# Rotating queries and keys straight out of PSUM and normalising them afterwards, with a shorter lag behind the products

## The chip, the cores and the metric

The kernel runs on one core of a Trainium2 chip, as one launch. The metric is the device time of the launch in microseconds (us). TensorE (PE in the profile) multiplies matrices out of SBUF into PSUM, which has eight banks of 512 f32 columns by 128 partitions; VectorE (DVE) and ScalarE (ACT) read PSUM and SBUF; GpSimd (POOL) works in SBUF; SyncE (SP) issues the DMAs.

## The reference

A two-layer encoder on 1024 tokens of width 1024, f32 throughout. Layer 0 mixes tokens by grouped-query attention (16 query heads, 4 key/value heads, 64 wide), layer 1 by a pooling mixer; each layer then has cross-attention to 256 memory tokens and a gated MLP. The change lies in the start of layer 0's attention alone:

```python
qkv = h @ w_qkv
q = rmsnorm(q, q_gain)            # per token and head: q * rsqrt(mean(q*q) + eps) * gain
k = rmsnorm(k, k_gain)
q = apply_axial_rope(q, cos, sin) * (HEAD_DIM ** -0.5)
k = apply_axial_rope(k, cos, sin) # out = stack([x1*c - x2*s, x2*c + x1*s])
scores = einsum(q, k); p = softmax(scores); o = einsum(p, v)
```

The norm of a token and head is one number per 64 values, so that it commutes with the rotation: rotating first and scaling afterwards gives the same up to rounding. The gains are folded into the cos and sin tables.

## The kernel before, in words

Every f32 product is made as three products of halves (a high part and a low part of each operand, `mm3`, lines 755 to 757), so each operand that goes into TensorE has to be split: ACT writes the high part (`high`, L668), DVE subtracts it from the source and writes the low part (`low`, L671).

The attention of layer 0 has two stages, each planned by its own `Plan`. A `Plan` is a list scheduler: each operation is added with an engine, a cost, what it reads, what buffers it takes from which pool, and a due time. The due time of a TensorE operation is the sum of the TensorE costs ahead of it; the operations before it are due by that much earlier than their own lag; `late` sets a due time by hand. The plan then simulates the engines and writes the instructions in the order in which they would start. TensorE's order is the one in which its operations were added. On the chip every engine runs its own queue in that order and waits by semaphores, so a wrong guess of the plan shows as a wait, never as another order.

The first stage (QKV) makes eight key/value tiles, K0 to K7 (128 tokens each; 24 products of 512 columns), then 32 query tiles (128 tokens by 256 columns, four heads; 24 products of 256 columns, `plan_gemm`). Its PSUM is a pool "B" of six banks for products and turns, and two banks "A". Eight "peaks" (`plan_peaks`: two score products into pA, and DVE's maximum over them, `nm`, L802) for the first group of the loop stand between the query tiles. The weights of the next four heads come as four pieces in two halves by DMA and are split by ACT and DVE (`plan_weights`).

What follows a key or query product is `plan_head` (L1010 to L1056) and a turn. In the kernel before:
- `square` on ACT (L1016): squares of the bank, scaled by `first`, the token's own norm, into `sq`;
- `reduce` on DVE (L1020): sums of 64 into `ss`;
- `rstd` on POOL: mean and eps (L728, `ms`) and the power -1/2 (L730, `rs`);
- `scaled` on DVE (L1033): bank times `first` times `rs`, into an SBUF buffer `qn` (a `kr` for keys). This is the last read of the bank;
- `crossed` on DVE (L1040, two instructions): the buffer with its pairs swapped, times the sin table, into `rb`;
- `straight` on DVE (L1044): the buffer times the cos table, in place;
- `both` on POOL (L1048): the sum of the two, in place;
- the `turn` on PE (L1105 for queries, L1072 for keys): two transposes (four for keys K2 and up, which also turn the difference `dk` of two key tiles, made on POOL, L1066) into another bank, then the split by ACT and DVE (`put`).

A turn stands `LAG` products behind its own product in TensorE's order. The last `LATE` query tiles are not turned in this stage: their rotated queries stay in an SBUF buffer `scr`, and the loop turns them (`plan_late`, L1213).

The second stage (the loop) has 16 groups of scores (PE L796 into pS and DVE's maximum L802 for the next group's softmax shift; L1239 into pT), exponentials on ACT (L1246) and products with the values (L1281), with sums on DVE (L1290) and POOL (L1293). It uses all eight banks again: pS is banks 0 to 2, pT 3 to 6, pO 7, so that its first products wait until the first stage has read those banks for the last time. After it come the output product, the cross-attentions, the pooling mixer and the MLPs, which the change does not touch; most of the time lies there.

## Time and profile before

| what | before |
|---|---|
| time, median of 3 runs | 2417.65 us (2416.79 to 2420.77) |
| the profiled execution: its time | 2417.89 us |
| the profiled execution: its span | 2416.1 us, granted TensorE clock 0.997 |
| TensorE busy | 2388.5 us, 99% |
| DVE, ACT, POOL busy | 1885.5, 1180.3, 415.3 us |
| key products and their turns | to about 60 us from the span's start |
| query products and their turns | about 60 to 163 us |
| the loop begins | 172.1 us |

All times of the profile count from the span's start. In a timeline a row is one instruction, or several like ones in a run (`x6`): its start, its length, the engine, the line, what it writes and reads, the sizes, and in brackets how long the engine sat idle before it and who released it. Two neighbouring rows of an engine may overlap a little, since the next instruction starts while the last one drains. In a table of groups a row gives busy time and the mean length of one, then idle time in front of them. In a table of windows each engine has its busy time and instruction count per stretch; PEclk is the granted clock of TensorE, 1.00 at full speed.

### The profile page before, as it was taken

To read this page: it belongs to the slowest core of one execution; us is meant where nothing else is said; L and a number is where in the kernel's file an instruction comes from. 1 tells how busy PE (TensorE), PEld (TensorE's weight loads), DVE (VectorE), ACT (ScalarE), POOL (GpSimd) and SP (SyncE) were. 2 spreads that over 40 slices of the span, in tenths; PEclk is the share of its full clock that TensorE was granted. 3 is DMA by queue.
4 is the path that set the end of the run, shared out by engine and by line. 5 is a ranking of instruction groups with operands and counts; after the bars stand their busy time and mean duration, and the time that the engine had idled before them with its cause. 6 is when DMAs were issued, how large, how long until landed. Compare 5 with 4: busy or idle time off the path is not lost.

```text
span 2416.1 us, 33574 instructions
## 1 busy us (share of the span) xinstructions
PE 2388.5 (99%) x12281; PEld 1925.2 (80%) x12281; DVE 1885.5 (78%) x2691; ACT 1180.3 (49%) x1900; POOL 415.3 (17%) x458
## 2 busy tenths in 40 slices
PE   9989999999999999999999999999999999999998
PEld 7974445688998888888888888798888888888887
DVE  6779999549873798888888767987389888888875
ACT  7225555425552465555554427555255554555542
POOL 5746777500020000000000003011000000000001
PEclk9999999999999999999999999999999999999999
DMA  6000001335961233333387533695123332338752
GB/s 247 8 1 10 19 15 44 120 105 175 319 223 40 72 116 114 105 109 109 96 271 260 178 108 129 207 323 217 49 87 111 108 109 87 112 121 273 261 187 101
DMA packets 323297, 323.00 MB, mean 134 GB/s; under 512 B 32596, under 2 KB 253628, under 8 KB 323132
## 3 DMA queue, kind: packets, MB, share of 16 engines
q1 hardware_dynamic: 323132, 320.85, 41.1%
q8 instruction: 97, 1.59, 0.3%
q14 instruction: 68, 0.56, 0.1%
HBM read 233.30 MB, written 82.64 MB: 131 GB/s over the span
## 4 chain that ended last, share of the span: by engine, by line
PE 91%; issue 3%; DVE 3%; POOL 2%; DMA 1%; ACT 1%; SPq 0%; POOLq 0%; DVEq 0%; ACTq 0%
PE pB L755 23%; PE pB L756 23%; PE pB L757 23%; PE pO L1281 4%; PE pT L1239 3%; PE pA L757 3%; PE pA L755 3%; PE pA L756 3%; PE pS L796 2%; PE pB L324 1%; DVE R L671 1%; PE pS L1317 1%; PE pA L2293 0%; POOL rs L730 0%; POOL scr L1293 0%
## 5 line engine op out<-in xcount | busy, mean ns | idle before, releaser
L756 PE MATMUL pB<-R,R 128*128 128x512 f32 (+1 forms) x2860 | 1051.8, 368 | 0.2 <-DVE R L671 0.2
L755 PE MATMUL pB<-R,R 128*128 128x512 f32 (+1 forms) x2732 | 1022.6, 374 | 2.2 <-ACT R L668 0.8
L757 PE MATMUL pB<-R,R 128*128 128x512 f32 (+1 forms) x2728 | 1014.8, 372 | 1.3 <-DVE R L671 1.2
L756 PEld LDWEIGHTS pB<-R,R 128*128 128x128 f32 x2860 | 538.9, 188 | 88.5 <-DVE R L671 1.2
L755 PEld LDWEIGHTS pB<-R,R 128*128 128x128 f32 x2732 | 514.6, 188 | 96.3 <-ACT R L668 2.0
L757 PEld LDWEIGHTS pB<-R,R 128*128 128x128 f32 x2728 | 513.8, 188 | 91.8 <-DVE R L671 3.0
L668 ACT ACTIVATE R<-scr 128x512 fp32r<-128x512 f32 (+3 forms) x376 | 269.5, 744 | 235.2 <-DMA scr<-Gs 62.1
L671 DVE TENSOR_TENSOR R<-scr,R 128x512 fp32r<-128x512 f32 (+2 forms) x336 | 289.5, 889 | 25.1 <-ACT R L668 24.3
L728 POOL TENSOR_SCALAR ms<-ss 128x1 f32<-128x1 f32 (+1 forms) x92 | 25.7, 279 | 1645.1 <-ACT R L736 1279.5
L671 DVE TENSOR_TENSOR R<-X,R 128x512 fp32r<-128x512 f32 x258 | 175.5, 688 | 48.3 <-ACT R L668 47.9
L668 ACT ACTIVATE R<-X 128x512 fp32r<-128x512 f32 x258 | 160.9, 630 | 97.8 <-PE pB L756 48.3
L438 ACT COPY scr<-pB 128x512 f32<-128x512 f32 x156 | 91.1, 584 | 181.8 <-PE pB L757 174.6
L802 DVE TENSOR_REDUCE nm<-pS 128x1 f32<-128x512 f32 x240 | 153.2, 683 | 19.8 <-PE pS L796 18.3
L1246 ACT ACTIVATE X<-pT 128x1024 f32<-128x1024 f32 x128 | 125.3, 1023 | 79.7 <-PE pT L1239 74.4
L755 PE MATMUL pA<-R,R 128*128 128x512 f32 (+1 forms) x420 | 150.6, 359 | 0.0
L757 PE MATMUL pA<-R,R 128*128 128x512 f32 (+1 forms) x420 | 150.3, 358 | 0.0
L756 PE MATMUL pA<-R,R 128*128 128x512 f32 (+1 forms) x420 | 150.0, 357 | 0.0
L1281 PE MATMUL pO<-X,XV 128*64 128x512 f32 x512 | 123.8, 605 | 0.0
L1984 DVE TENSOR_TENSOR X<-pB,X 128x512 f32<-128x512 f32 (+1 forms) x109 | 74.7, 686 | 62.1 <-PE pB L757 61.3
L440 DVE TENSOR_TENSOR scr<-pB,scr 128x512 f32<-128x512 f32 x156 | 107.1, 687 | 11.8 <-PE pB L757 11.5
L1239 PE MATMUL pT<-R,R 64*128 64x512 f32 x768 | 105.5, 395 | 1.6 <-ACT X L1246 1.6
L1829 DVE SCALAR_TENSOR_TENSOR scr<-scr,conv 128x1023 f32<-128x1023 f32 x66 | 84.7, 1284 | 20.5 <-ACT scr L1824 18.6
(222 smaller groups left out, 2936.0 us busy)
## 6 DMA issues: line engine op xcount, KB each, us to landing
Gs<-X SPq DMA_DIRECT2D x105, 256.0 KB
X<-in_ffn_w_up SPq DMA_DIRECT2D x51, 512.0 KB
scr<-in_ffn_w_down SPq DMA_DIRECT2D x45, 512.0 KB
scr<-Gs SPq DMA_DIRECT2D x35, 512.0 KB
scr<-in_xattn_w_kv SPq DMA_DIRECT2D x32, 512.0 KB
scr<-Gs SPq DMA_DIRECT2D x42, 384.0 KB
XV<-in_ffn_w_up SPq DMA_DIRECT2D x31, 512.0 KB
Wt<-scr SPq DMA_DIRECT2D x44, 256.0 KB
```

Source lines behind the costliest of these rows:

```text
L438: self.nc.scalar.copy(out, p)
L440: self.nc.vector.tensor_tensor(out=out, in0=p, in1=out, op=OP.add)
L668: self.nc.scalar.activation(hi, src, AF.Copy)
L671: self.nc.vector.tensor_tensor(out=lo, in0=src, in1=hi.bitcast(F32), op=OP.subtract)
L755: mm(out, ah, bh, start=start, stop=False)
L756: mm(out, ah, bl, start=False, stop=False)
L757: mm(out, al, bh, start=False, stop=stop)
L802: nc.vector.tensor_reduce(NM[G][:, 2 * n + x.start:2 * n + x.stop], S, axis=AX.X, op=OP.max, negate=True)
L1239: nc.tensor.matmul(T[G, kt % 2][:, x * 512:(x + 1) * 512], left, right, start=first and (i, j) == (0, 0), stop=shifted or (not first and i ...
L1246: nc.scalar.activation(E[G, kt], T[G, kt % 2], AF.Exp)
L1281: nc.tensor.matmul(O[G][x * HD:(x + 1) * HD], V32[kt // 4][:, kt % 4, m // 4 * 2 + x], E[G, kt][:, x * 512:(x + 1) * 512], start=kt == 0, ...
L1829: nc.vector.scalar_tensor_tensor(c[:, 1:], u[:, :S - 1], self.cv[:, 0, j + f:j + f + 1], c[:, 1:], op0=OP.mult, op1=OP.add)
```

## The change

1. The head of a tile is put in another order. `crossed` and `straight` now read the product's bank (two sin products into `rb`, one cos product into `qn`), `both` adds them on POOL, and `scaled` comes last, in SBUF and in place, with `first` and `rs`. The bank is now read for the last time by `straight`, which does not wait for the norm. The mean and eps are made on DVE (`mean`, L727) instead of POOL; POOL keeps the power (L735) and the addition (L1052).
2. A turn stands three products behind its product (`LAG` 3).
3. Two query tiles instead of four are left to the loop (`LATE` 2): the first stage has 30 turns of queries instead of 28. For the two that are left, `scaled` too is done by the loop.
4. The peaks stand behind query tiles 5, 7, 9, 11, 13, 16, 22 and 25, counted from 0 (before: 10, 12, ... 24).
5. The low parts of the second halves of weight pieces 2 and 3 go from DVE to POOL (L974, 128x1024).
6. Due times and costs: the splits behind a query's turn get `late`, the loop's plan starts with the engines as busy as the first plan left them, the late tiles get other known times.

```diff
-QKV = (... QS[:9], *(it for n, q in enumerate(QS[9:]) for it in ([q, ("S", n // 2)] if n % 2 == 1 and n < 16 else [q])))
-LAG, LATE = 4, 4
+PEAKS = (5, 7, 9, 11, 13, 16, 22, 25)
+QKV = (... *(it for n, q in enumerate(QS) for it in ([q, ("S", PEAKS.index(n))] if n in PEAKS else [q])))
+LAG, LATE = 3, 2
...
+    def mean(self, on, ss, n, width):
+        ms = self.stat(n, "ms")[:ss.shape[0]]
+        on.tensor_scalar(ms, ss, 1.0 / width, EPS, op0=OP.mult, op1=OP.add)
+        return ms
...
-                    def low(raw=raw, g=g):
-                        self.low(h[:, 4 * g:4 * g + 4], l[:, 4 * g:4 * g + 4], at[raw])
+                    kind, engine = ("pool", nc.gpsimd) if g and piece > 1 else ("add", nc.vector)
+                    def low(raw=raw, g=g, engine=engine):
+                        engine.tensor_tensor(out=l[...], in0=at[raw], in1=h[...].bitcast(F32), op=OP.subtract)
...
                 def reduce():
                     nc.vector.tensor_reduce(at[ss], ...)
+                    at[ss] = self.mean(nc.vector, at[ss], 4, HD)
...
-                def scaled():
-                    nc.vector.scalar_tensor_tensor(q3(), x, first[:, t:t + 1], r, op0=OP.mult, op1=OP.mult)
                 def crossed():
-                    q5, b5 = (... for z in (at[qn], at[rb]))
+                    q5, b5 = (... for z in (at[b], at[rb]))
                 def straight():
-                    nc.vector.tensor_tensor(out=q3(), in0=q3(), in1=tabs[kind][:, t, 0]..., op=OP.mult)
+                    nc.vector.tensor_tensor(out=q3(), in0=at[b]..., in1=tabs[kind][:, t, 0]..., op=OP.mult)
+                def scaled(at=at):
+                    z = at[qn].rearrange("p (h c) -> p h c", h=4)
+                    nc.vector.scalar_tensor_tensor(z, z, first[:, t:t + 1], at[ss]..., op0=OP.mult, op1=OP.mult)
-                plan.add("add", 340, reduce, [sq], [ss], uses=[sq])
-                plan.add("scale", 2.9, rstd, [ss], [ss])
-                plan.add("add", 340, scaled, [b, ss], [qn], ..., [b])
-                plan.add("add", 490, crossed, [qn, tabkey], [rb], [("rb", rb)], [qn, *used])
-                plan.add("add", 360, straight, [qn, tabkey], [qn], uses=[qn, *used])
-                plan.add("scale", 2.4, both, [qn, rb], [qn] + ..., uses=[qn, rb])
+                plan.add("add", 490, crossed, [b, tabkey], [rb], [("rb", rb)], [b, *used])
+                plan.add("add", 400, straight, [b, tabkey, rb], [qn], ..., [b, *used])
+                plan.add("add", 440, reduce, [sq], [ss], uses=[sq])
+                plan.add("scale", 2.3, rstd, [ss], [ss], late=3.0 if deferred else None)
+                plan.add("scale", 1.7, both, [qn, rb], [qn], uses=[qn, rb], late=4.0 if deferred else None)
+                if deferred:
+                    finish[late.index(it)] = scaled
+                else:
+                    plan.add("add", 340, scaled, [qn, ss, ("first", t)], [qn] + ..., uses=[qn])
...
-            plan = Plan(R, {}, {"A": 3, "B": 2, "O": 1, ...})
+            plan = Plan(R, plan.over, {"A": 3, "B": 2, "O": 1, ...})
-            plan.known.update({("late", i): 3.0 + 2.5 * i for i in range(LATE)})
+            plan.known.update({("late", i): (0.5, 3.0)[max(i - LATE + 2, 0)] for i in range(LATE)})
+                plan.add("add", 340, lambda: at_late.update({i: finish[i]()}), [b], [b], uses=["late"], late=1.0)
                 plan.add("turn", 2, turn, [b], [(b, 0)], [("A", b)], ["late"])
```

Three places show what the order of instructions becomes. In the rows a number behind a name tells one buffer from another; pB, pS and pT are PSUM banks, sq, ms, rs, qn, kr, rb and scr are SBUF buffers.

The first is TensorE at the end of the first stage. Before, the last product goes to pB_2200, one turn follows, and the loop begins with pS_2303:

```order
L756 MATMUL pB_2200<-R5_72,R16_83 128x256
L757 MATMUL pB_2200<-R4_71,R17_84 128x256
L1105 MATMUL pB_2225<-ident_87,qn_2119 128x128 x2
L796 MATMUL pS_2303<-R0_67,R18_85 128x512
L796 MATMUL pS_2304<-R0_67,R18_85 128x512
L1239 MATMUL pT_2307<-R18_85,R0_67 128x512 x4
```

In the changed kernel the last product goes to pB_2224, two turns follow, and the loop begins with pS_2313:

```order
L761 MATMUL pB_2224<-R5_72,R16_83 128x256
L762 MATMUL pB_2224<-R4_71,R17_84 128x256
L1117 MATMUL pB_2265<-ident_87,qn_2168 128x128 x2
L1117 MATMUL pB_2270<-ident_87,qn_2217 128x128 x2
L801 MATMUL pS_2313<-R0_67,R18_85 128x512
L801 MATMUL pS_2314<-R0_67,R18_85 128x512
```

Two turns in place of one stand between the last product and the loop. By the placement of the banks pS_2303 lies in that of pB_2200, and waits for its `scaled`; pS_2313 lies in that of the last turn, pB_2270, and waits for its `low`, and pS_2314 in that of the last product, pB_2224.

The second is VectorE at the same place. Before, from the last tile's `reduce` (sq_2244) to the first maximum of the loop:

```order
L1020 TENSOR_REDUCE ss4_2246<-sq_2244 128x4
L671 TENSOR_TENSOR R11_78<-pB_2225,R11_78 128x2x128
L1033 SCALAR_TENSOR_TENSOR scr_2170<-pB_2127,first_113,rs_2253 128x256
L1040 TENSOR_TENSOR rb_2256<-scr_2170,tab_111 128x8x16 x2
L1044 TENSOR_TENSOR scr_2170<-scr_2170,tab_111 128x256
L1033 SCALAR_TENSOR_TENSOR scr_2170<-pB_2172,first_113,rs_2263 128x256
L1040 TENSOR_TENSOR rb_2266<-scr_2170,tab_111 128x8x16 x2
L1044 TENSOR_TENSOR scr_2170<-scr_2170,tab_111 128x256
L1033 SCALAR_TENSOR_TENSOR scr_2170<-pB_2200,first_113,rs_2273 128x256
L1040 TENSOR_TENSOR rb_2276<-scr_2170,tab_111 128x8x16 x2
L1044 TENSOR_TENSOR scr_2170<-scr_2170,tab_111 128x256
L802 TENSOR_REDUCE nm_2314<-pS_2303 128x1
```

In the changed kernel, the same stretch, from the last tile's `reduce` (sq_2268):

```order
L1027 TENSOR_REDUCE ss4_2276<-sq_2268 128x4
L727 TENSOR_SCALAR ms_2278<-ss4_2276 128x4
L1038 TENSOR_TENSOR rb_2282<-pB_2224,tab_111 128x8x16 x2
L672 TENSOR_TENSOR R12_79<-pB_2265,R12_79 128x2x128
L1048 TENSOR_TENSOR scr_2273<-pB_2224,tab_111 128x256
L672 TENSOR_TENSOR R12_79<-pB_2270,R12_79 128x2x128
L1211 MEMSET ones_2309 128x64
L807 TENSOR_REDUCE nm_2327<-pS_2313 128x1
```

The three `scaled` that stood behind the last `reduce`, each on an `rs` of its own from POOL, are gone from this place; two of them (of pB_2173 and pB_2224) stand twelve maxima later, in the loop. Two `low` of turns have come in.

The third is POOL in the key tiles: the tables for the keys (scr, from tab and gk), the powers rs of the first tiles, the first tokens' norms (first), and the first sums kr. Before:

```order
L899 TENSOR_TENSOR scr_370<-tab_111,gk_115 128x8x64
L906 TENSOR_TENSOR scr_370<-tab_111,gk_115 128x8x16 x2
L728 TENSOR_SCALAR ms_381<-ss4_368 128x4
L730 TENSOR_TENSOR rs_383<-ms_381,mh_92 128x4
L931 TENSOR_SCALAR ms_390<-ss_387 128x1
L932 TENSOR_TENSOR first_113<-ms_390,mh_92 128x1
L728 TENSOR_SCALAR ms_393<-ss4_377 128x4
L730 TENSOR_TENSOR rs_395<-ms_393,mh_92 128x4
L906 TENSOR_TENSOR scr_370<-tab_111,gk_115 128x8x16 x2
L1048 TENSOR_TENSOR kr_397<-kr_397,rb_438 128x256
```

In the changed kernel:

```order
L904 TENSOR_TENSOR scr_333<-tab_111,gk_115 128x8x64
L911 TENSOR_TENSOR scr_333<-tab_111,gk_115 128x8x16 x2
L936 TENSOR_SCALAR ms_373<-ss_370 128x1
L937 TENSOR_TENSOR first_113<-ms_373,mh_92 128x1
L911 TENSOR_TENSOR scr_333<-tab_111,gk_115 128x8x16 x2
L735 TENSOR_TENSOR rs_380<-ms_339,mh_92 128x4
L936 TENSOR_SCALAR ms_398<-ss_395 128x1
L937 TENSOR_TENSOR first_113<-ms_398,mh_92 128x1
L1052 TENSOR_TENSOR kr_389<-kr_389,rb_382 128x256
```

The tables now stand ahead of the first power, since `crossed` and `straight` need them before `scaled` needs the norm. On TensorE the first key tile's turn stands behind product K2 (before: behind K3, together with K1's).

More of the change, by code (lines that the diff above doesn't have):

```diff
@@ L40 @@
 QS = [(g, t) for g in range(2) for t in range(NT)] + [(2 + n // 4 % 2, n % 4 + n // 8 * 4) for n in range(2 * NT)]
[L41 to L42 removed]
+PEAKS = (5, 7, 9, 11, 13, 16, 22, 25)
+QKV = (*(("K", t) for t in range(NT)), *(it for n, q in enumerate(QS) for it in ([q, ("S", PEAKS.index(n))] if n in PEAKS else [q])))
+LAG, LATE = 3, 2
 QN = 4
@@ L779, in attention @@
         Q, OT, NM, ring = {}, [], {}, []
-        late = [(1, NKV - 1, t) for t in range(NT - LATE, NT)]
+        late, finish = [(1, NKV - 1, t) for t in range(NT - LATE, NT)], {}
         def rows(x):
@@ L1200, in attention @@
             T, E, O, acc, ON, RS = {}, {}, {}, {}, {}, {}
-            plan = Plan(R, {}, {"A": 3, "B": 2, "O": 1, "pt": 6, "scr": 6, "qm": 3, "half": len(R.freed)})
+            plan = Plan(R, plan.over, {"A": 3, "B": 2, "O": 1, "pt": 6, "scr": 6, "qm": 3, "half": len(R.freed)})
             plan.hold("qm", ("qm", 0))
```

43 lines of the change are left out of this document (22 added, 21 removed).

## The prediction

> **What bounds the kernel now.** I read the page first, then what TensorE waits for, then the stretch around the longest wait.
>
> ```profile
> PE 2388.5 (99%) x12281; PEld 1925.2 (80%) x12281; DVE 1885.5 (78%) x2691; ACT 1180.3 (49%) x1900; POOL 415.3 (17%) x458
> core 0: 2416.1 us, clock 0.997
> PE pS L796 <- DVE scr L1033: 9.0, 1, 9.0
> PE pB L1072 <- POOL dk L1066: 1.6, 2, 1.1
> PE pB L1190 <- POOL ident masks.py:199: 1.3, 1, 1.3
> PE pB L1072 <- POOL kr L1048: 0.6, 1, 0.6
> PE pS L796 <- DVE nm L802: 0.6, 2, 0.3
> ```
>
> TensorE is busy for all but 27.6 us of the span (2416.1 - 2388.5). The change leaves nearly all its matmuls in place, so it can win or lose only through TensorE's idle time, its granted clock, and a few turns. The last five rows are TensorE's waits (total, times, longest), four up to the start of the loop and one in its first 68 us: one of 9.0 us between the two stages, and 2.2 us on the keys (1.6 + 0.6). The wait for ident stands ahead of the first product and is not touched. The wait of 9.0 us in order of time, on TensorE, POOL and DVE:
>
> ```profile
> 162.73 0.38 PE L1105 MATMUL pB<-ident,qn 128*128 128x128 f32 x2
> 172.09 0.80 PE L796 MATMUL pS<-R,R 64*128 64x512 f32 x2 [8.97 <-DVE scr L1033]
> 166.73 1.01 POOL L730 TENSOR_TENSOR rs<-ms,mh 128x4 f32<-128x4 f32 x1
> 167.78 0.48 DVE L1033 SCALAR_TENSOR_TENSOR scr<-pB,first,rs 128x256 f32<-128x256 f32 x1 [2.21 <-POOL rs L730]
> 170.41 1.01 POOL L730 TENSOR_TENSOR rs<-ms,mh 128x4 f32<-128x4 f32 x1
> 171.46 0.48 DVE L1033 SCALAR_TENSOR_TENSOR scr<-pB,first,rs 128x256 f32<-128x256 f32 x1 [2.21 <-POOL rs L730]
> ```
>
> POOL and DVE hand the left-over tiles to each other, one per 3.68 us (171.46 - 167.78), and the loop's first bank is free only when the last `scaled` has read it. What the idle time does to the clock:
>
> ```profile
> 164.50:165.00 0.50, 0.00 (x0) 0.00 (x0) 0.47 (x3) 0.00 (x0) 0.00 (x0) 1.00 0.00 0
> 165.00:165.50 0.50, 0.00 (x0) 0.00 (x0) 0.47 (x2) 0.00 (x0) 0.00 (x0) 0.53 0.00 0
> 175.00:175.25 0.25, 0.25 (x5) 0.18 (x4) 0.23 (x1) 0.25 (x1) 0.00 (x0) 0.50 0.00 0
> 175.50:176.00 0.50, 0.50 (x8) 0.42 (x4) 0.50 (x2) 0.15 (x1) 0.00 (x0) 1.00 0.00 0
> 180.00:200.00 20.00, 19.57 (x111) 9.32 (x110) 18.75 (x29) 9.55 (x13) 8.76 (x4) 1.00 0.04 1
> ```
>
> The columns are length, busy PE, PEld, DVE, ACT, POOL, then the clock. It falls to 0.50 at about 165.0, 1.9 us after the last turn's end (162.73 + 0.38), and is full again at about 175.3, 3.2 us into the loop.
>
> **The change, part by part. The gap between the stages.** The durations of the new chain come from these rows (the first three from the old tail, the fourth a turn from the chain of waits, the others means over 62 to 160 us; L808 is the nearest row to the new `mean`, a DVE instruction on 8 columns):
>
> ```profile
> 162.61 0.29 PE L757 MATMUL pB<-R,R 128*128 128x256 f32 x1
> 162.94 0.47 ACT L1016 ACTIVATE sq<-pB,first 128x256 f32<-128x256 f32 x1 [2.34 <-PE pB L757]
> 163.44 0.42 DVE L1020 TENSOR_REDUCE ss<-sq 128x4 f32<-128x256 f32 x1 [2.33 <-ACT sq L1016]
> 159.81 0.22 PE pB L1105 x2
> L1040 DVE TENSOR_TENSOR rb<-qn,tab 128x128 f32<-128x128 f32 x56 | 15.1, 312 | 0.0
> L1044 DVE TENSOR_TENSOR qn<-qn,tab 128x256 f32<-128x256 f32 x28 | 12.4, 444 | 0.3
> L671 DVE TENSOR_TENSOR R<-pB,R 128x256 fp32r<-128x256 f32 x29 | 12.1, 416 | 0.0
> L808 DVE TENSOR_TENSOR nmr<-nm 128x8 fp32r<-128x8 f32 x1 | 0.2, 172 | 0.0
> L802 DVE TENSOR_REDUCE nm<-pA 128x2 f32<-128x1024 f32 x8 | 9.7, 1217 | 2.1 <-PE pA L796 2.1
> ```
>
> The last product ends at 162.90 (162.61 + 0.29); the loop begins 9.19 us later (172.09). In the new order, counted from the end of the last product: `square` and the start of `reduce` at 0.54 (163.44 - 162.90), `reduce` to 0.96, `mean` 0.17 to 1.15, `crossed` about 0.55 (two of 0.31 that overlap) to 1.7, a `low` 0.37, `straight` 0.42, the last `low` 0.42: 2.9 us. No step waits for POOL: the power is needed by `scaled` alone, which stands in the loop. `straight` out of PSUM is priced by L671, the same size with one operand in PSUM (416 ns), and `crossed` by the old SBUF form; both could come out between 0.8 and 1.3 of that, which is -0.2 to +0.3 us here. One more turn stands ahead of the last product's end: 30 instead of 28 in all, two behind it instead of one. A turn delays TensorE by 0.22 us. So the gap saves 9.19 - 2.9 - 0.22 = 6.1 us. Ends: 6.6 if `low` does not bind, 4.0 if DVE reaches the end one tile late (2.1 us). The second turn's operand must be scaled by then: by the same durations its `scaled` ends about 0.4 us ahead of the last product's end, thin, but what it would cost is tenths.
>
> **The clock.** The loop's first 3.2 us run at half speed. Two shapes give the loss: six pT matmuls took 1.51 us at 172.66 and 1.10 at 174.79, and five took 0.96 at full clock. Some of it is hidden by DVE, which is the busier engine there. I take 0.7 us, from 0.4 for one such group to 1.2 for three. Is it saved? The new idle time is 2.4 us (2.9 less two turns). Two idle times in this trace stand on either side of it:
>
> ```profile
> 172.66 1.51 PE L1239 MATMUL pT<-R,R 64*128 64x512 f32 x6
> 174.79 1.10 PE L1239 MATMUL pT<-R,R 64*128 64x512 f32 x6
> 177.12 0.96 PE L1239 MATMUL pT<-R,R 64*128 64x512 f32 x5
> 446.63 0.96 PE L1239 MATMUL pT<-R,R 64*128 64x512 f32 x6 [1.56 <-ACT X L1246]
> 450.00:452.00 2.00, 2.00 (x12) 0.71 (x10) 1.66 (x2) 0.58 (x1) 0.58 (x1) 1.00 0.81 258
> ```
>
> 1.56 us at 446 left the clock at 1.00; at 165.0 it fell after 1.9 us. 2.4 is above both, so a fall is likelier than not, and then the loop's first 3 us are as slow as before: I take nothing saved, and 0.7 us as the other end. The Trainium skill, page "TensorE: Matmul & The Clock Gate", section "What's actually happening", says that the clock halves after an idle window of about 3.4 us, counted by a free-running window. Read as 3.4 us of idleness, 2.4 us would leave the clock alone and the sum would be 0.7 us lower; the measured 1.9 us disagrees with that reading, and I go by the measurement.
>
> **The loop.** It turns two tiles less: two turns moved to the first stage, where the one ahead of the last product's end is already paid and the other lies in the gap. In the loop they cost TensorE about 0.22 us each; DVE, the fuller engine of 180 to 200 (18.75 of 20 us), loses two `low` (0.83 us) and one `crossed` and `straight` that ran beside the loop's first products (0.9), and gains two `scaled` (0.96). I take 0.5 us saved, between 0 and 1. The rest of the loop keeps its order but for numbers of buffers and one place on POOL in the second group; I price that at nothing, since POOL is 17% busy, and up to 1 us if an exponential waits for it.
>
> **The keys.** The chain of a key tile becomes sum, `scaled`, difference, turn; the power is off it unless it is late. The old waits sum to 2.2 us. The first key's turn moves ahead by one product (5.4 us), to about 27.3, and needs POOL's tables, which ended late before:
>
> ```profile
> 26.09 0.55 POOL L932 TENSOR_TENSOR first<-ms,mh 128x1 f32<-128x1 f32 x1
> 30.37 0.86 POOL L1048 TENSOR_TENSOR kr<-kr,rb 128x256 f32<-128x256 f32 x1 [1.50 <-DVE kr L1044]
> 33.73 0.44 PE L1072 MATMUL pB<-ident,kr 128*128 128x128 f32 x2 [0.61 <-POOL kr L1048]
> ```
>
> In the new order the sum of the first key stands right behind that `first` (26.64): 0.75 for the sum, 0.48 for `scaled`, 27.9 us: a wait of about 0.6. If one of the table's instructions comes 2 to 3 us later the wait is 3. I take 0.9 us of waits in all in place of 2.2: 1.3 saved, between 2.2 saved and 3 lost.
>
> **The query tiles.** Here TensorE did not wait, and should not now. A tile takes TensorE 3.1 us. DVE needs per tile 0.41 + 0.17 + 0.55 + 0.44 + 0.42 + 0.48 = 2.5 us, and 1.22 more for a peak, which comes every second tile from 5 to 13 and brings TensorE 0.5 us of its own: 6.2 of 6.7 us, or 93%. That is what DVE had before in its fullest stretch, without a wait:
>
> ```profile
> 100.00:130.00 30.00, 30.00 (x240) 27.95 (x239) 27.88 (x62) 8.62 (x20) 23.01 (x33) 1.00 0.00 1
> 102.72 1.05 POOL L821 TENSOR_SCALAR R<-ident 128x1024 fp32r<-128x1024 f32 x1
> 103.18 0.94 DVE L1040 TENSOR_TENSOR rb<-qn,tab 128x128 f32<-128x128 f32 x2
> L1048 POOL TENSOR_TENSOR qn<-qn,rb 128x256 f32<-128x256 f32 x28 | 20.9, 746 | 0.9 <-DVE qn L1044 0.4 <-PE pB L756 0.4
> 188.14 2.38 POOL L1293 TENSOR_TENSOR scr<-scr 128x1024 f32<-128x1024 f32 x1 [14.41 <-DVE scr L1290]
> ```
>
> From the end of a product to the end of its `scaled` I count about 6.4 us (its turn's neighbours on ACT 1.2, `crossed` and `straight` 1.4, the sums and powers of the tile before and its own, one period later, 3.8); the turn is due after three periods, 9.3. The slack of 2.9 us covers two `low` of weights still on DVE (1.22 each) and the two on POOL, which should take the 2.4 us of L1293, the same shape. I cost it at nothing; the cover is that slack, and DVE's place at 93%.
>
> **Sum.** -6.1 - 0 - 0.5 - 1.3 = -7.9 us against the profiled execution's 2417.89 (span 2416.1), which is 0.24 above the median of 2417.65: 2410.0 us, or 0.32% below the median. A measurement of this kernel tells about 0.2% from no change, 4.8 us.
>
> **The rivals.**
> - The clock stays full. The fall at 165.0 needs idleness that the new gap lacks, and the 0.7 us are saved too: 2409.3. The Trainium skill's window, in the section named above, would give this where it straddles the gap.
> - Turns wait. With a lag of three, `scaled` at the end of the chain and DVE at 93%, the turn finds its operand unfinished. Against it: 2.9 us of slack. For it: `mean` is new on DVE, and the forms out of PSUM are not in this trace. It begins where a tile costs DVE over 2.7 us in the dense stretch; from there each turn waits for the excess. 0.3 us at each of 30 turns is 9 us: 2419.0. It ends on the slower side from 0.45 us a turn on (13.5 us: 2423.5).
> - DVE and POOL hold each other up. At 103.18 the two `crossed` took 0.94 us in place of 0.55 (2 of 0.31, overlapping), beside POOL's 1.05 us instruction. If `scaled`, now in SBUF, waits for each of the two `low` of weights on POOL (2.4 us each) where DVE is full, 4.8 us come back: 2414.8. The Trainium skill, page "SBUF — State Buffer", section "Who interferes with whom", states that a DVE instruction with two SBUF inputs and a GpSimd instruction that reads SBUF exclude each other. The row at 103.18 agrees. But per tile three such DVE instructions become one, so it should rather help; hence a small chance.
> - The keys: the tables are 3 us late at the first turn and the other waits stay. Then 1.3 saved becomes 3 lost: 2414.3.
> - The gain is given back in the loop: its first steps hang on DVE (94% in 180 to 200), so that an earlier start only makes TensorE wait for maxima. All but about 2.5 us (the keys and part of the gap) would be lost: 2415.4. Against it: TensorE waited for maxima 0.6 us in its first 68 us.
>
> **How the numbers follow.** The forecast's case has 0.45, the full clock 0.20, DVE with POOL 0.04, the keys 0.08, the loop 0.08, waiting turns 0.15, of which 0.06 stay under 0.3 us a turn and 0.08 exceed 0.45. The forecast's own range is 2407 (the best ends of gap, loop and keys: -6.6 - 1 - 2.2 and 0.7 for the clock) to 2412.5 (4.0 gained in the gap, 0.5 in the loop, 1 on the keys). The range 2406 to 2418 takes in all but the waits from 0.3 us a turn on. Faster by over 0.2% (below 2412.8): the first two cases and some of the keys, the loop and mild waits, 0.71. Within 0.2% (to 2422.5): 0.20. Slower: 0.09.
>
> **What would show it.** In the changed trace: the wait of the first pS matmul at about 2.4 us instead of 9.0, released by a DVE `low`; PEclk 0.50 for some 3 us around the loop's start, or 1.00 by the first rival; DVE's rows between the last `reduce` and the first maximum without idle time for POOL; no waits at L1117 between 62 and 160; under 1 us in all on the key turns; the loop's start at about 164.7. I am wrong if turns of queries wait, if `crossed` and `straight` out of PSUM take over 1.3 times the rows above, or if the loop's first 30 us get longer.

## The result, and the profile after

| | before | after |
|---|---|---|
| median of six runs each, same chips | 2419.15 us (2416.15 to 2421.53) | 2408.68 us (2407.75 to 2412.04) |
| ratio | | 0.9960, 95% interval 0.9947 to 0.9973 |
| span of the profiled execution | 2416.1 us | 2406.0 us |

The change takes 0.40% off (0.27 to 0.53%). The forecast was 2410.0 us, 0.32% below the median known then. The busy times on the changed kernel's page:

```profile
PE 2386.1 (99%) x12281; PEld 1924.6 (80%) x12281; DVE 1894.9 (79%) x2729; ACT 1179.0 (49%) x1900; POOL 407.2 (17%) x420
```

What its TensorE waits for up to the start of the loop (total, times, longest):

```profile
PE pS L801 <- DVE R L672: 2.4, 1, 2.4
PE pB L1202 <- POOL ident masks.py:199: 1.3, 1, 1.3
PE pB L1084 <- DVE kr L1056: 0.3, 1, 0.3
PE pB L1117 <- DVE qn L1056: 0.2, 1, 0.2
```

The wait of 9.0 us between the stages is one of 2.4, and a `low` (L672) releases it, no longer a `scaled`. The keys' waits fell from 2.2 us to 0.3. The timeline of TensorE at that place: the last product, the two turns and the loop's first product.

```profile
160.75 0.29 PE L762 MATMUL pB<-R,R 128*128 128x256 f32 x1
160.87 0.38 PE L1117 MATMUL pB<-ident,qn 128*128 128x128 f32 x2
161.47 0.41 PE L1117 MATMUL pB<-ident,qn 128*128 128x128 f32 x2 [0.22 <-DVE qn L1056]
164.25 0.49 PE L801 MATMUL pS<-R,R 64*128 64x512 f32 x2 [2.37 <-DVE R L672]
```

And that of DVE, its row of work around the last `reduce`:

```profile
161.57 0.41 DVE L1048 TENSOR_TENSOR scr<-pB,tab 128x256 f32<-128x256 f32 x1
161.91 0.41 DVE L1027 TENSOR_REDUCE ss<-sq 128x4 f32<-128x256 f32 x1
162.35 0.47 DVE L727 TENSOR_SCALAR ms<-ss 128x4 f32<-128x4 f32 x1
162.73 0.48 DVE L1038 TENSOR_TENSOR rb<-pB,tab 128x128 f32<-128x128 f32 x2
163.13 0.41 DVE L672 TENSOR_TENSOR R<-pB,R 128x256 fp32r<-128x256 f32 x1
163.46 0.41 DVE L1048 TENSOR_TENSOR scr<-pB,tab 128x256 f32<-128x256 f32 x1
163.79 0.41 DVE L672 TENSOR_TENSOR R<-pB,R 128x256 fp32r<-128x256 f32 x1
```

DVE works without a break and waits for POOL nowhere in this row. The last product ends at 161.04 (160.75 + 0.29) and the loop begins at 164.25, 3.21 us later (9.19 before). The chain begins at 161.57 with a `straight` of the tile before, so that `reduce` starts 0.33 us later than its square would let it.

Where the 10.1 us of the two spans went, by points of the timelines: the end of the last product, then the starts of the loop's first pT product (scores) and of its 64th, 97th, 489th and 497th of 512 pO products (with the values), and the end:

| point | before | after | gained up to here |
|---|---|---|---|
| end of the last product | 162.90 | 161.04 | 1.86 |
| first pT product | 172.66 | 164.59 | 8.07 |
| 64th pO product | 215.28 | 204.78 | 10.50 |
| 97th pO product | 234.91 | 225.80 | 9.11 |
| 489th pO product | 441.38 | 431.89 | 9.49 |
| 497th pO product | 447.52 | 437.70 | 9.82 |
| end of the span | 2416.1 | 2406.0 | 10.1 |

So 1.9 us came ahead of the gap and 6.2 in it. The loop's first 40 us brought 2.4, but 1.4 of that was given back by the 97th pO. TensorE's timeline of the changed kernel shows a wait for a maximum there, where the kernel before has none:

```profile
212.18 0.50 PE L801 MATMUL pS<-R,R 64*128 64x512 f32 x1 [0.84 <-DVE nm L807]
```

From one run of pO products to the next it is 5.23 us there (207.37 to 212.60), 3.92 before (217.87 to 221.79). Another 1.0 us came back in three steps, 0.4 before the 489th pO, 0.3 at the 497th and 0.3 behind it.

### The profile page after: what moved, and what is told of

It reads as the page before. It is cut to its first block, busy times and chain, and to the rows that moved or that the text cites. A ratio compares the mean times of both kernels' runs of the same rounds, so it can differ in the third digit from the quotient of the medians.

```text
span 2406.0 us, 33540 instructions
## 1 busy us (share of the span) xinstructions
PE 2386.1 (99%) x12281; PEld 1924.6 (80%) x12281; DVE 1894.9 (79%) x2729; ACT 1179.0 (49%) x1900; POOL 407.2 (17%) x420
## 4 chain that ended last, share of the span: by engine, by line
PE 91%; DVE 3%; issue 3%; DMA 1%; POOL 1%; ACT 1%; SPq 0%; POOLq 0%; DVEq 0%; ACTq 0%
PE pB L760 23%; PE pB L762 23%; PE pB L761 23%; PE pO L1296 5%; PE pT L1254 4%; PE pA L762 3%; PE pA L760 3%; PE pA L761 3%; PE pS L801 2%; PE pB L325 1%; DVE R L672 1%; PE pS L1332 1%; DMA scr<-in_ffn_w_down 0%; PE pA L2308 0%; POOL rs L735 0%
## 5 line engine op out<-in xcount | busy, mean ns | idle before, releaser
L672 DVE TENSOR_TENSOR R<-scr,R 128x512 fp32r<-128x512 f32 (+2 forms) x332 | 283.4, 881 | 26.7 <-ACT R L669 25.8
L727 POOL TENSOR_SCALAR ms<-ss 128x1 f32<-128x1 f32 x52 | 13.2, 253 | 1628.4 <-ACT R L741 1279.9
L672 DVE TENSOR_TENSOR R<-X,R 128x512 fp32r<-128x512 f32 x258 | 175.0, 686 | 48.3 <-ACT R L669 48.0
L669 ACT ACTIVATE R<-pB 128x256 fp32r<-128x256 f32 (+1 forms) x139 | 64.9, 482 | 118.5 <-PE pB L1117 62.7
```

Source lines behind the costliest of these rows:

```text
L669: self.nc.scalar.activation(hi, src, AF.Copy)
L672: self.nc.vector.tensor_tensor(out=lo, in0=src, in1=hi.bitcast(F32), op=OP.subtract)
```

## The experiments

The key figures of all kernels, in us from the timelines and the waits of one profiled execution each, and the ratio to the kernel before over the runs of the same chip. The span of the kernel before is from an execution (2417.89 us) 1 to 2 us faster than its medians on these chips (2419.15 to 2420.11), so kernels are compared by the ratio rather than by the span.

| kernel | waits of key turns | last product ends | first pT | 64th pO | span | ratio, 95% interval |
|---|---|---|---|---|---|---|
| before | 2.2 | 162.90 | 172.66 | 215.28 | 2416.1 | |
| after | 0.3 | 161.04 | 164.59 | 204.78 | 2406.0 | 0.9960 (0.9947 to 0.9973) |
| after, once more | 0.4 | 160.88 | 164.66 | 205.84 | 2406.5 | 0.9953 (0.9938 to 0.9968) |
| new head alone | 2.1 | 162.80 | 165.84 | 212.89 | 2413.7 | 0.9977 (0.9966 to 0.9988) |
| after, four tiles left | 1.6 | 162.60 | 164.92 | 210.44 | 2412.1 | 0.9969 (0.9958 to 0.9981) |
| after, old head | 2.1 | 163.82 | 171.30 | 219.29 | 2606.8 | 1.0778 (1.0762 to 1.0794) |
| after, old head, free start | 2.7 | 164.31 | 171.79 | 214.31 | 2414.2 | 0.9993 (0.9983 to 1.0003) |
| before, gap filled | 2.3 | 163.09 | 172.63 | 214.38 | 2415.3 | 0.9986 (0.9977 to 0.9996) |
| after, sum of the last tile later | 0.6 | 161.47 | 164.55 | 204.82 | 2405.6 | 0.9953 (0.9938 to 0.9967) |
| after, `straight` twice | 1.0 | 163.00 | 167.24 | 208.57 | 2416.0 | 0.9974 (0.9965 to 0.9983) |
| after, mean on POOL | 2.7 | 163.45 | 166.98 | 208.43 | 2411.1 | 0.9970 (0.9959 to 0.9982) |
| after, lag 4 | 1.4 | 162.20 | 165.65 | 207.49 | 2409.0 | 0.9964 (0.9951 to 0.9977) |
| after, old peaks | 1.1 | 161.69 | 164.91 | 206.03 | 2407.5 | 0.9955 (0.9940 to 0.9969) |
| after, weights on DVE | 0.8 | 163.04 | 166.65 | 208.35 | 2409.5 | 0.9961 (0.9947 to 0.9976) |

### The new head alone

The kernel before with the new `plan_head` and with `scaled` of the left-over tiles in the loop; lag 4, four tiles left, and all else as before.

```diff
 LAG, LATE = 4, 4
-                plan.add("add", 340, scaled, [b, ss], [qn], ...)      # the old head
+                plan.add("add", 490, crossed, [b, tabkey], ...)       # the new head, as in the change
...
+                plan.add("add", 340, lambda: at_late.update({i: finish[i]()}), [b], [b], uses=["late"], late=1.0)
```

> The kernel before with the new head alone: bank read by the rotations, mean on DVE, scaled last; lag 4, four tiles left to the loop, peaks, weight halves and due times as before. Theory A (the gap came from POOL's power standing between a bank and its last read): the gap from the last product's end to the first pS or pT product falls from 9.19 us to about 3.0, the key waits from 2.2 to under 1, so 6 to 8 us less than before, most of the whole change. Rival B (the gap is short because only two tiles are left behind the last product): the gap stays at 8 us or more and the time within 2 us of before.

The gap closes: 3.03 us from the last product to the first pT (165.84 - 162.80; 9.76 before). Theory A holds there. The key waits did not fall (2.1 us), and most of the rest was lost in the loop: from the first pT to the 64th pO it took 47.1 us, against 42.6 before. TensorE's waits say why (the second row is the gap):

```profile
PE pS L1224 <- DVE scr L1053: 2.5, 1, 2.5
PE pT L1251 <- DVE R L671: 2.0, 1, 2.0
```

The last of four late turns (L1224) waits 2.5 us for its `scaled`, which DVE does behind its maxima, and behind that wait the granted clock is 0.50 from 193.4 to 196.9. So the head gives the gap, but the time is 0.23% less and not 0.4%: about 5 us by the medians, where 6 to 8 were expected.

### Four tiles left to the loop

```diff
-LAG, LATE = 3, 2
+LAG, LATE = 3, 4
```

> The changed kernel with four instead of two query tiles left to the loop, all else as changed. Theory A: the gap does not grow, since no left-over tile waits for POOL there; with no turn behind the last product it is about 2.1 us (3.21 with two), TensorE has two turns less ahead of it (0.44), and the loop pays 0.2 to 0.6 us for each of the two more turns: within 1 us of the changed kernel. Rival B: each further left-over tile adds 3.7 us as it did before: 7 us slower.

The gap is shorter, 2.32 us to the first pT, as expected without a turn behind the last product, and no 3.7 us per tile come back: rival B falls. But theory A's price for the late tiles was too low. The last late turn waits 2.5 us here too, and from the first pT to the 64th pO the loop takes 45.5 us against 40.2 and 41.2 in the two executions of the changed kernel. Of the 5.3 us more than in the first of these, 3.6 are left at the 489th pO; part of them is a half clock behind that wait (0.50 from 191.5 to 194.9). The whole is 2 to 4 us slower than the changed kernel, by ratios whose intervals overlap. Two late tiles instead of four thus belong to the gain with the new head, through the loop and not through the gap. TensorE's waits (the second is the gap):

```profile
PE pS L1227 <- DVE scr L1056: 2.5, 1, 2.5
PE pS L801 <- DVE ones L1211: 1.9, 1, 1.9
```

And DVE's timeline at the `scaled` that the last late turn waits for; it, too, stands behind maxima and takes twice its time:

```profile
188.39 1.87 DVE L807 TENSOR_REDUCE nm<-pS 128x1 f32<-128x512 f32 x3
190.19 1.04 DVE L1056 SCALAR_TENSOR_TENSOR scr<-scr,first,rs 128x256 f32<-128x256 f32 x1
```

### The old head in the changed kernel

The order and the engines of the old head; lag 3, two tiles left, peaks, weight halves and due times as changed.

```diff
 LAG, LATE = 3, 2
-                plan.add("add", 490, crossed, [b, tabkey], ...)       # the new head
+                plan.add("add", 340, scaled, [b, ss], [qn], ...)      # the old head
-                plan.add("add", 340, lambda: at_late.update({i: finish[i]()}), ...)
```

> The changed kernel with the old head (norm out of PSUM first, mean on POOL, rotations in SBUF), everything else as changed: lag 3, two tiles left to the loop, peaks, weight halves, due times. Theory A: after the last product two tiles still pass from POOL to DVE one after the other, so the loop's pT waits about 5 us, the key waits of 2 us are back, and some turns of queries wait too, since the old chain takes longer: 4 to 8 us slower than the changed kernel. Rival B: the gap is about 3 us and the time within 1 us of the changed kernel.

It took 2608.11 us, ratio 1.0778 (1.0762 to 1.0794), which neither theory expected. The waits of TensorE over the whole kernel:

```profile
PE pT L1248 <- DMA R<-nmr: 134.6, 26, 9.4
PE pT L1248 <- DVE scr L1040: 5.5, 1, 5.5
```

The second row is the gap as theory A has it. The first lies in the loop, where the head has no part. In DVE's timeline the first reciprocal of a group's sums stands late:

```profile
236.96 0.93 DVE L1339 RECIPROCAL rs<-rs 8x128 f32<-8x128 f32 x1
```

The next kernel differs only in the start of the loop's plan:

```diff
-            plan = Plan(R, plan.over, {"A": 3, "B": 2, "O": 1, ...})
+            plan = Plan(R, {}, {"A": 3, "B": 2, "O": 1, ...})
```

> The changed kernel with the old head, and with the loop's plan started as before the change (all engines free) instead of from where the first plan left them. It separates two things in the last old-head kernel, which lost 135 us in the loop waiting for the DMAs that carry nmr. Theory A: that loss came from the loop's plan, which was started with DVE and POOL busy for long and put each group's reciprocal two maxima later; with a free start it is gone, and what is left is the gap (pT waits about 5.5 us for scaled) and 2 us on keys: 4 to 6 us slower than the changed kernel, 4 to 6 faster than before. Rival B: the loss in the loop comes from the head's tiles themselves and stays: over 2500 us.

The loss is gone; the same reciprocal in this kernel's timeline:

```profile
209.91 0.93 DVE L1339 RECIPROCAL rs<-rs 8x128 f32<-8x128 f32 x1
```

The wait for `scaled` stays, by TensorE's waits:

```profile
PE pT L1248 <- DVE scr L1040: 5.5, 1, 5.5
PE pB L1079 <- POOL kr L1055: 1.8, 1, 1.8
```

Theory A is right on the cause of the 135 us; a mean clock of 0.962 instead of 0.998 is part of the 190 us that the kernel lost in all. Its total is not met: the kernel is as fast as the one before (0.9993, 0.9983 to 1.0003), where it should have been 4 to 6 us faster, since the keys wait 2.7 us and the gap to the first pT is 7.48 (171.79 - 164.31; 171.30 - 163.82 in the kernel with the old head alone). Lag, peaks, weight halves, due times and fewer left-over tiles without the new head are worth nothing that can be measured.

### What the half clock costs

```diff
                 for _, f in todo:
                     if f:
                         f()
+                def fill():
+                    spare = self.psA()
+                    for _ in range(75):
+                        nc.tensor.transpose(spare[:, :P], self.ident, self.ident)
+                plan.add("turn", 1, fill, (), ["spare"], [("A", "spare")], ["spare"])
```

> The kernel before with 75 transposes more, on a spare bank, put on TensorE behind the last turn of the first stage: they end before the loop can begin, so that the wait is filled with work and the clock should not fall. It tells what the half clock of the loop's first 3.2 us costs. My term: the loop begins when it did, and the time is 0.7 us less than before (0.4 to 1.2). If DVE hides it all: no change. If the half clock costs all that the changed kernel won behind the loop's start beyond the two turns: 1.2 to 1.7 us less.

TensorE's idle time shrinks to 0.8 us, the first pT comes when it did (172.63), and the clock is full there. The windows of this kernel:

```profile
170.00:172.00 2.00, 1.50 (x14) 1.25 (x12) 0.31 (x1) 0.00 (x0) 1.49 (x3) 1.00 0.00 0
172.00:173.00 1.00, 0.68 (x6) 0.68 (x8) 0.93 (x4) 0.00 (x0) 0.00 (x0) 1.00 0.00 0
```

The 64th pO comes 0.87 us sooner behind the first pT (41.75 against 42.62), in the range that was given, and the 489th 1.36 us sooner (267.36 against 268.72), which is above it. Then TensorE of the kernel with the gap filled waits 1.89 us for an exponential, and behind that its clock falls:

```profile
445.57 1.04 PE L1245 MATMUL pT<-R,R 64*128 64x512 f32 x6 [1.89 <-ACT X L1252]
446.54 3.94 PE L1287 MATMUL pO<-X,XV 128*64 128x512 f32 x10
```

The granted clock is 0.50 from 446.3 to 449.8, and ten pO products take 3.94 us, where sixteen took 3.65 at 447.52 before. At the 501st pO only 0.1 us is left of the lead (448.30 against 448.43). So in this execution one half clock was saved and another was paid. The spans differ by 0.8 us, the medians by 3.2 (0.9986, 0.9977 to 0.9996): the profiled execution of the kernel before took 2417.89 us, 2.2 less than that kernel's median of 2420.11 on the chip of this experiment, which is nearly all of that difference.

### The changed kernel once more

No edit.

> The changed kernel once more, unaltered, for another execution's profile. If the clock's window runs free against the kernel, an idle time of 2.4 us falls into one window in some executions and over two in others: a mean clock of 0.999 without a fall, 0.998 with one, and the executions with a fall 1 to 3 us slower. The key waits (0.3 us in the first profile, 1.6 in one with the same order of the keys) differ between executions too, by 0.3 to 1.6.

The same idle time, 2.37 us, and this time the clock fell. The windows of the first execution, then of this one:

```profile
163.00:164.00 1.00, 0.00 (x0) 0.00 (x0) 1.00 (x5) 0.00 (x0) 1.00 (x2) 1.00 0.00 0
165.00:166.00 1.00, 1.00 (x11) 0.85 (x11) 1.00 (x3) 0.20 (x1) 0.00 (x0) 1.00 0.00 0
```

```profile
163.00:164.00 1.00, 0.00 (x0) 0.00 (x0) 1.00 (x5) 0.00 (x0) 1.00 (x2) 0.75 0.00 0
165.00:166.00 1.00, 1.00 (x8) 0.72 (x6) 1.00 (x2) 0.00 (x0) 0.00 (x0) 0.50 0.00 0
166.00:167.00 1.00, 1.00 (x8) 0.81 (x6) 0.19 (x1) 0.30 (x1) 0.00 (x0) 0.54 0.00 0
167.00:168.00 1.00, 1.00 (x11) 0.79 (x8) 0.97 (x2) 0.74 (x2) 0.00 (x0) 1.00 0.00 0
```

The fall lasts from 163.5 (0.75 on the mean of 163 to 164) to about 166.9. It makes the loop's first part 1.0 us longer (41.2 against 40.2), of which 0.8 is left at the 489th pO. There the first execution waits 1.23 us for an exponential and this one 0.64, which leaves 0.3; the spans differ by 0.5. The "1 to 3 us" of the expectation are more than these two traces show, and of this kernel's four runs the profiled one, with its fall, was the fastest (2408.25; the others 2408.89 to 2410.34). Nor does the mean clock tell a fall: four other kernels (mean on POOL, lag 4, old peaks, weights on DVE) have one at the gap and a mean of 0.999. The key waits were nearly the same here (0.4), so that half of the expectation is not borne out by this pair; the 1.6 us with four tiles left has the same order of instructions in the keys.

### What the query turns have in hand

```diff
+                    nc.vector.tensor_tensor(out=q3(), in0=at[b]..., in1=tabs[kind][:, t, 0]..., op=OP.mult)
                     nc.vector.tensor_tensor(out=q3(), in0=at[b]..., in1=tabs[kind][:, t, 0]..., op=OP.mult)
```

> The changed kernel with the cos product of every tile made twice, the second time over the first with the same values: 0.4 us more on DVE for each of 40 tiles. The prediction's claim (2.9 us of slack between scaled and its turn, DVE at 2.5 us of 3.1 per tile): no waits of query turns, 0.4 to 0.8 us more in the gap, 1 us slower in all. What the changed trace says (scaled took 758 ns instead of 482, a tile costs DVE 2.7 us, and the slack falls from 4 us to 0.3 at the eighteenth turn): DVE then needs some 7 us more than TensorE has over the 30 tiles, 4 of them covered, so turns wait 3 to 8 us in all.

Query turns waited 1.4 us in all, which lies between the two readings: more than the prediction's none, less than 3. The span is 10 us longer, the median of the runs only 4 (2412.93): the profiled execution lies at the upper end of the runs. Up to the first pT it is 2.65 us behind the changed kernel (167.24 against 164.59), of which 1.4 are the turns' waits and 0.7 the gap. Behind the loop it lost another 4.6 us, where its instructions are the same. Of these, 2.6 come between 1440 and 1460 us, where it waits 1.26 us for a `low` and the granted clock is then 0.50 from 1456.7 to 1460.1; another 1.1 come at 2217, where TensorE waits 1.8 for a `low`. The rest is spread, and why these waits were longer stays open.

```diff
                     at[ss] = self.stat(4, "ss4")
-                    at[ss] = self.mean(nc.vector, at[ss], 4, HD)
...
-                    at[ss] = self.rstd(at[ss], 4, HD, at[ss])
+                    at[ss] = self.rstd(at[ss], 4, HD)                 # the mean on POOL again
```

> The changed kernel with the mean and eps back on POOL, in front of each power, all else as changed. DVE loses 0.23 us per tile. Theory A: the gap falls by the mean (0.47 in the changed trace) to about 2.8 us, the turns' slack grows, and the time falls by 0.3 to 0.6 us. Rival B: POOL's chain decides, the power comes 0.2 to 0.3 us later for each tile and the turns at the end wait that much longer: no change or up to 0.5 us slower.

The gap falls to 2.93 us up to the first pS (166.38 - 163.45), near theory A's 2.8, but both theories miss the time: it is 2.5 to 4 us slower than the changed kernel (0.9970 against 0.9960 and 0.9953; the intervals overlap). A tile's chain passes through POOL, and one more instruction there delays it. TensorE's waits:

```profile
PE pB L1083 <- POOL dk L1077: 1.5, 2, 1.2
PE pB L1083 <- DVE kr L1055: 1.2, 1, 1.2
PE pB L1116 <- DVE qn L1055: 1.1, 1, 1.1
```

The keys wait 2.7 us (0.3 in the changed kernel), and the last turn 1.1 (0.2): the sign that rival B gave, with a size that was too small. So the mean on DVE, which the prediction had as a cost on DVE, keeps waits off the keys and the last turn.

### Lag, peaks, weights, and the last tile's sum

```diff
-LAG, LATE = 3, 2
+LAG, LATE = 4, 2
```

> The changed kernel with a lag of four products instead of three, all else as changed. It tells what the shorter lag is worth. For the shorter lag: one turn (0.22 us) and one low (0.33 us) more stand behind the last product, so the gap grows by about 0.5 us, and the first key's turn goes back behind K3, so that key waits of about 2 us return as in the kernel with the new head alone: 1 to 3 us slower. Against it (the longer slack, 3 us more for each query's turn, is worth more than that): up to 0.5 us faster.

Key waits are 1.4 us, the gap to the first pT 3.45 (no growth), one query turn waits 0.5, and the runs are 1 to 3 us slower (0.9964, 0.9951 to 0.9977): as expected of the shorter lag, except in the gap, though the intervals overlap and don't settle it.

```diff
-PEAKS = (5, 7, 9, 11, 13, 16, 22, 25)
+PEAKS = (10, 12, 14, 16, 18, 20, 22, 24)
```

> The changed kernel with the peaks where they were, behind query tiles 10, 12 ... 24, all else as changed. If their place matters: eight maxima of 1.22 us stand later, the slack of the turns, which fell to 0.3 us at the eighteenth turn, falls to nothing, and turns wait 0.5 to 3 us in all. If not: within 0.5 us in the query tiles, and the time within 1 us of the changed kernel.

No difference in the time (0.9955, 0.9940 to 0.9969), no wait in the query tiles: the place of the peaks does nothing here.

```diff
-                    kind, engine = ("pool", nc.gpsimd) if g and piece > 1 else ("add", nc.vector)
+                    kind, engine = "add", nc.vector
```

> The changed kernel with the two low parts of the weights back on DVE (1.22 us each there, 2.4 and 2.6 on POOL), all else as changed. If the move to POOL was needed: 2.4 us more on DVE where the slack is least, turns wait 0.5 to 2.5 us. If POOL's long instruction is as bad for DVE as the work itself, since scaled waits for it: no difference, within 0.5 us in the query tiles.

One query turn waits 0.9 us at 127.7, and the last product ends 2 us later than in the changed kernel; the runs are 1 to 2 us slower, though the intervals overlap (0.9947 to 0.9976 against 0.9938 to 0.9968). The wait is the sign that was expected if the move to POOL was needed; the time alone does not show it.

```diff
-                plan.add("scale", 2.3, rstd, [ss], [ss], late=3.0 if deferred else None)
+                plan.add("scale", 2.3, rstd, [ss], [ss], late=12.0 if it == late[-1] else 3.0 if deferred else None)
```

> The changed kernel with the sum, mean and power of the last tile due later (12 instead of 3 us behind the plan's end), so that its reduce and mean stand behind the last low of the turns and no longer ahead of it, and its square behind the two splits on ACT. Theory A (the gap of 3.21 us is DVE's row of work behind the last product): the gap falls by reduce and mean, 0.75 us, to about 2.45, and the time by 0.75. Rival B (the gap is set by the turn's put on ACT or by the last turn's operand): under 0.3 us.

The gap falls from 3.55 to 3.08 us to the first pT, two thirds of what theory A gave, and more than rival B allowed. The time is the changed kernel's (0.9953, 0.9938 to 0.9967): half a microsecond is below what the runs tell apart.

## Why the prediction was right

**The gap.** Right in mechanism and size. 2.9 us were forecast from the last product to the loop, 3.21 measured; saved 5.76 (9.19 - 3.21, less 0.22 for the turn ahead), against 6.1. The 0.3 us more are the `straight` that stands ahead of `reduce` (0.33); from there to the loop it took 2.34 us, 2.36 forecast, since a `mean` of 0.47 instead of 0.17 was made up by rows that came out shorter. The second turn's operand, called thin, was 0.28 us late, and the turn waited 0.22. The two kernels that swap the head alone show the cause: up to the first pT the new head closes the gap in the old kernel from 9.76 us to 3.03, and the old one opens it in the new from 3.55 to 7.48.

**The keys.** 1.3 us forecast, 1.9 measured (2.2 less 0.3), inside its ends. The first key's `scaled` ended at 27.6 us (27.9 forecast) and its turn waited 0.3. What I took for an effect of the head is none by itself: with the new head alone the keys wait 2.1 us. Nor is it one of the lag by itself, with 2.1 and 2.7 for the old head at lag 3. With both, and the mean on DVE, they waited 0.3 to 1.6 us, so that 0.3 is the best of seven executions. Which order of instructions makes the difference was not isolated.

**The clock.** My likeliest case, that it falls again, held in the second execution and not in the first; of the eight profiled executions with the new head and two tiles left, six had a fall at the gap. By the Trainium skill, page "TensorE: Matmul & The Clock Gate", section "What's actually happening", the gate judges by a free-running window of some 3.4 us. The traces agree: 2.37 us of idleness do both, and each single fall lasts 3.4 us. Nothing here shows where the window's edges lay. So the length of an idle time, by which I placed 2.4 us between 1.56 and 1.9, does not decide: the clock also fell behind a wait of 1.26 us (with one of 0.31 shortly before it) at 1456.7 in the kernel with `straight` twice, and did not behind one of 1.92 in the gap of the kernel with the last tile's sum later. The price was somewhat low: 0.7 forecast, with an upper end of 1.2; 0.9 and 1.0 at the 64th pO, and 1.4 and 0.8 at the 489th.

**The loop.** "I take 0.5 us saved, between 0 and 1" holds at the end of the loop, at its lower bound, and not at its beginning. Between the kernel with the gap filled (four late tiles, full clock) and the changed one (two, full clock) the way from the first pT to the 64th pO shrinks by 1.6 us (41.75 to 40.19), but by 0.2 to the 97th and by 0.1 to the 489th (267.36 to 267.30): the wait for a maximum at 212.18 takes it back. That is the rival of a gain given back in the loop, on a small scale. This pair also differs in the head. With the new head in both, two more late tiles cost 5.3 us at the 64th pO and 3.6 at the 489th, a half clock included: I counted a tile's turn and its rows on DVE, and not that its `scaled` stands behind DVE's maxima. I also called DVE the fuller engine of 180 to 200; the row that I cited has TensorE busy for 19.57 us and DVE for 18.75.

**The query tiles.** Right in the result, wrong in the working. The steps that failed are the 2.5 us that a tile was to cost DVE and the slack of 2.9 us. The changed kernel's groups of DVE over 58 to 161 us:

```profile
L1056 DVE SCALAR_TENSOR_TENSOR qn<-qn,first,rs 128x256 f32<-128x256 f32 x30 | 22.7, 758 | 10.0 <-POOL qn L1052 5.3 <-POOL rs L735 4.8
L1038 DVE TENSOR_TENSOR rb<-pB,tab 128x128 f32<-128x128 f32 x62 | 14.9, 280 | 0.0
L1048 DVE TENSOR_TENSOR qn<-pB,tab 128x256 f32<-128x256 f32 x30 | 12.4, 414 | 0.0
```

Its timeline at the `scaled` of the eighteenth query tile, on DVE, and the `both` beside it on POOL:

```profile
124.54 0.96 DVE L1056 SCALAR_TENSOR_TENSOR qn<-qn,first,rs 128x256 f32<-128x256 f32 x1 [0.41 <-POOL rs L735]
124.48 0.74 POOL L1052 TENSOR_TENSOR qn<-qn,rb 128x256 f32<-128x256 f32 x1
```

And the turn of that tile on TensorE:

```profile
125.78 0.38 PE L1117 MATMUL pB<-ident,qn 128*128 128x128 f32 x2
```

The rotations out of PSUM are a little faster than before (280 against 312 ns, 414 against 444), but `scaled` takes 758 ns on the mean instead of 482: in SBUF it runs beside the `both` of the next tile, as at 124.54, where it took 0.96. A tile costs DVE 2.7 us, the size from which the rival of waiting turns was to begin. The slack, from the end of `scaled` to the start of its turn, is 4.0 us at the first turn and 0.28 at the eighteenth (125.78 - 124.54 - 0.96); I had 2.9 for all. Two kernels show that it was nearly used up: with the mean on POOL the last turn waits 1.1 us, with the weights on DVE one waits 0.9. The rival of waiting turns was nearer than its 0.15 says; that no turn waited inside the stage was in part luck.

**DVE and POOL.** The rival happened at the first of the two `low` of weights on POOL, and cost no wait: the `scaled` at 85.33 took 2.17 us beside it, and the slack of its turn, still 1.9 us, covered it. DVE's and POOL's timeline:

```profile
84.83 2.40 POOL L974 TENSOR_TENSOR R<-scr,T 128x1024 fp32r<-128x1024 f32 x1 [1.11 <-ACT T L669]
85.33 2.17 DVE L1056 SCALAR_TENSOR_TENSOR qn<-qn,first,rs 128x256 f32<-128x256 f32 x1
```

The sentence "per tile three such DVE instructions become one, so it should rather help" failed: these instructions and `scaled` sum to 1.73 us a tile (2 x 280, 414, 758 ns), 1.55 before (2 x 312, 444, 482), since 15 of the 30 `scaled` took over 0.6 us, each of them beside a POOL instruction, mostly the next tile's `both`.

**The sum.** -10.1 us of span against -7.9. Of the 2.2 us between them 0.7 lie ahead of the loop (8.07 against 6.1 + 1.3, the keys most of it), 0.9 in the loop up to its 489th pO (1.42 against 0.5), 0.3 at the 497th, where a wait for an exponential is 1.23 us instead of 1.56, and 0.3 behind the loop. The 0.9 go with the clock that did not fall: in the second execution, where it did, the same stretch saves 0.6 (268.72 to 268.14). So the mechanism of the first execution was that of the rival with the full clock (0.20); the second was the forecast's own case, with a time of 2408.25 us in the same range.

## What to carry to other kernels

Look for what reads a PSUM bank last, and move what waits for another engine behind that read: a scale that commutes with the rest can be applied in SBUF, where nobody waits for the bank. At a border between stages count the work behind the last product engine by engine, in the order of their queues; here that count came out to 0.3 us. A planner that carries its engines' end times into the next plan can spoil it: the same loop cost 190 us more when it was started with them from another head.

## What the runs showed of the hardware

- An idle time of 2.37 us on TensorE halved its clock in one execution of a kernel and not in another; the half clock lasted 3.4 us.
- `scaled`, with both operands in SBUF, took two to four and a half times its 0.48 us (0.96, 1.50, 2.17) where it began just behind a POOL addition, multiplication or `low` (0.74, 1.29, 2.40). The one in the keys; DVE's and POOL's timeline:

```profile
30.28 1.50 DVE L1056 SCALAR_TENSOR_TENSOR kr<-kr,first,rs 128x256 f32<-128x256 f32 x1 [0.64 <-POOL kr L1052]
30.20 1.29 POOL L904 TENSOR_TENSOR tab<-tab,gq 128x512 f32<-128x512 f32 x1
```

The Trainium skill, page "SBUF — State Buffer", section "Who interferes with whom", has the rule, that such a pair shuts each other out; these rows agree with it, since in all three pairs the DVE instruction ends 0.3 us behind the POOL one. Beside POOL's power (128x4), which reads SBUF too, the same instruction kept its time, so that the rule is not borne out there:

```profile
160.84 0.48 DVE L1056 SCALAR_TENSOR_TENSOR qn<-qn,first,rs 128x256 f32<-128x256 f32 x1 [0.70 <-POOL qn L1052]
160.76 1.01 POOL L735 TENSOR_TENSOR rs<-ms,mh 128x4 f32<-128x4 f32 x1
```
